# Delta rule of a gated DeltaNet layer: keys and queries of a sample sequence against its states in one 32-column matmul, and the keys' scale on VectorE

## The chip, the cores and the metric

One Trainium2 chip, of which the program uses one core. A core has TensorE (matmuls; loading the stationary operand is shown apart), VectorE, ScalarE, GpSimd and SyncE, each with its own instruction stream, an on-chip memory of 128 partitions (SBUF) and an accumulator memory for matmul results (PSUM, in banks). The metric is the device time of one execution in microseconds (us); lower is better.

## The reference, cut to what matters

Two decoder layers are run for a prompt (1 sequence of 256 positions) and for 8 sample sequences of 4 positions each, which share the weights. The first layer mixes by retention, the second by a gated delta rule; each is followed by a convolutional feed-forward layer. The change lies in the delta rule alone. For one chunk of it:

```python
q = jnp.repeat(l2norm(q), rep, axis=2) * GDN_DK ** -0.5      # 8 key heads, 16 value heads, 128 wide
k = jnp.repeat(l2norm(k), rep, axis=2)
...
G = jnp.cumsum(gc, axis=-1)
dG = G[..., :, None] - G[..., None, :]
decay = jnp.exp(jnp.where(tri_incl, dG, -jnp.inf))
kb = kc * bc[..., None]
L = jnp.where(tri_strict, jnp.einsum('bhid,bhjd->bhij', kb, kc) * decay, 0.0)
rhs = jnp.concatenate([vc * bc[..., None], kb * jnp.exp(G)[..., None]], axis=-1)
sol = lax.linalg.triangular_solve(eye + L, rhs, left_side=True, lower=True, unit_diagonal=True)
u, w = sol[..., :dv], sol[..., dv:]
v_new = u - jnp.einsum('bhid,bhdv->bhiv', w, S)
attn = jnp.einsum('bhid,bhjd->bhij', qc, kc) * decay
o = jnp.einsum('bhid,bhdv->bhiv', qc * jnp.exp(G)[..., None], S) + jnp.einsum('bhij,bhjv->bhiv', attn, v_new)
S = S * jnp.exp(G_last)[..., None, None] + jnp.einsum('bhjd,bhjv->bhdv', kc * jnp.exp(G_last[..., None] - G)[..., None], v_new)
```

The prompt starts from zero states; each of the 8 sample sequences brings its own 128 x 128 state for each of the 16 value heads, and its 4 positions are one chunk.

## The kernel before, in words

**Stages.** The program runs the retention layer, its feed-forward layer, the delta-rule layer (`gdn`), the second feed-forward layer and an end. The delta-rule layer takes about 580 to 985 us of the profiled span. The activations of all 288 positions (256 of the prompt, then 32 of the samples: 8 sequences by 4) stand as columns, so a projection is a chain of matmuls `128x128` by `128x288`, in three passes (`whi` by high part, `whi` by low part, `wlo` by high part), all recorded under the line of `product` (L535). The weights come by DMA, ScalarE rounds them (`whi`, L416) and VectorE makes the rest (`wlo`, L417).

**Order.** The 16 value heads go in four head groups g = 0 to 3, of 4 value heads and 2 key heads. A written list gives the order of the groups' projections: keys and queries (K), values (V), output gate (Z) and output product (D, whose matmuls are called `down`), as `K0 V0 K1 A0 Z0 V1 K2 Z1 V2 K3 D0 V3 Z2 D1 D2 Z3 D3`. Beside it run side tasks, generators that are moved on by one step after every 6 matmuls of a projection (`QUANTUM`). They do the scores, the triangular inverse, the values, the samples and the states. So the side work of one group lies between the projection matmuls of others, and a scheduler then orders the instructions of each engine. TensorE runs its stream in that order: when a side matmul waits, the projection matmuls behind it wait too.

**The steps that the change touches.** `gdn_gates` runs once: it makes the log decays and their sums `pg` by small matmuls, `exs` by an exponential on ScalarE, and `nexg`, the negative of 4 of its columns, by one VectorE instruction (L1096). `gdn_kq` copies each group's sample keys (s = 0) and queries (s = 1) to `kqd`, once for each value head (L1147, GpSimd). `gdn_norms` makes the inverse norms `krs` (L557 is the last instruction of the inverse root, VectorE), then the product `knm` (L1187, VectorE), and the keys' scale `ksc`, beta over the squared norm: 4 GpSimd instructions (L1194) and a fifth for its negative (L1195). `gdn_scores` reads `ksc` first at `gnn` (L1291, VectorE): it multiplies the key scores `pa` (TensorE, L1288, twice for a group) by scale and decay. The second `pa` is put in the same banks and waits for the readers of the first, of which the last are called `gat` (L1295, L1296).

`gdn_samples` handles the 8 sample sequences of a group. The 32 sample columns are position times 8 plus sequence. It spreads the keys and the queries into 8 matrices that hold one sequence's 4 columns and zeros elsewhere (`bigs`, L1462, 4 GpSimd products with a mask of 128x256), so that each matmul writes all 32 columns' rows and the sum over the 8 sequences puts each row right. The states `gS` come by DMA, two sequences at a time. For each sequence bb, for keys and queries (s) and for each of 4 value heads (v) there is one matmul `pks` (L1479):

```python
pks[32 * v : 32 * v + 32, s * P : (s + 1) * P], lhsT=kqm[s][:, v // 2, bb, :], rhs=S[bb // 2][:, bb % 2, v, :]
```

It is 8 x 2 x 4 = 64 matmuls for a group, in 4 bursts of 16. Then `r` is made from the half of the keys (L1486, VectorE, all of this called `t` in the profile) and `qg` from the half of the queries (L1488, ScalarE). Three rounds follow of a small matmul `psy` (L1493) and a VectorE sum. `pks`, `psy` and two more tiles (tag "c") share one PSUM bank, so the first `psy` waits until `r` and `qg` have read `pks`.

`gdn_finish` normalises the outputs: `ro` by the inverse root and `qs` (4 GpSimd instructions at L1621 and one at L1622), `bigc` from it (L1631, VectorE, twice), then the state product `gpS` (L1636, TensorE, 4 matmuls, in one of the two banks of tag "b"). The samples' output is transposed by TensorE (`pxs`, L1660).

Of the kernel before, what the change touches and what calls it, by code (L numbers as in the profile page):

```python
# [295 lines left out]
class Program:  # L296
# [725 lines left out]
    def gdn_gates(self, hs):  # L1022
# [4 lines left out]
        baT = self.big([P, T], F32, "s", 512, 3, 1)[0:32]  # L1027
# [715 lines left out]
```

## Time and profile before

| | us |
|---|---|
| three runs | 1225.26, 1239.33, 1236.23 (median 1236.23) |
| the profiled execution | 1233.65 |
| its span in the trace | 1231.9 |
| TensorE, VectorE, ScalarE, GpSimd busy | 1164.1 (95%), 870.3 (71%), 608.8 (49%), 327.7 (27%) |
| mean granted clock of TensorE, as a share of full speed | 0.972 |

The span lies within the profiled execution's own time; 1.75 us lie around it. Busy times overlap, since the engines run side by side. A matmul in fp32 has two records in the trace, so 64 `pks` of a group are 128 records. Rows of a timeline give start, length, engine, line, operation, output and inputs, and in brackets how long the engine had stood idle just before, and what ended that.

### The profile page before, as it was taken

How to read it: one execution, taken by the hardware profiler on the slowest of the kernel's cores; microseconds unless marked ns; L12 is line 12 of the kernel's file. 1: busy time of each engine (PE TensorE's matmuls, PEld its weight loads, DVE VectorE, ACT ScalarE, POOL GpSimd, SP SyncE). 2: the span in 40 equal slices, each digit the busy share in tenths (PEclk: the TensorE clock that was granted, in tenths of full speed). 3: DMA queues.
4: the chain of work that ended last, by engine and by line, in shares of the span. 5: the costliest groups of instructions: out<-in, count | busy, mean ns of one | idle time of the engine just before them, and what ended most of it. 6: DMA issues, size and time to landing. Idle time of an engine off the chain costs nothing.

```text
span 1231.9 us, 24934 instructions
## 1 busy us (share of the span) xinstructions
PE 1164.1 (95%) x9486; PEld 1049.1 (85%) x9486; DVE 870.3 (71%) x2003; ACT 608.8 (49%) x1256; POOL 327.7 (27%) x507
## 2 busy tenths in 40 slices
PE   6999999999999999999989998988899899999996
PEld 2879798797969999997777788977889699999996
DVE  3657574765766666667679888797965588777775
ACT  2444534344445544444674645744544365555553
POOL 0213142251302122222252223233222113223232
PEclk9999999999999999999999988988989899999998
DMA  9998696877699556557636641533434897777621
GB/s 365 345 332 324 227 336 233 313 246 242 211 314 393 189 171 190 171 181 259 209 92 211 223 144 63 159 129 115 131 103 129 298 357 239 258 254 253 196 76 56
DMA packets 97480, 269.08 MB, mean 218 GB/s; under 512 B 26816, under 2 KB 29088, under 8 KB 97232
## 3 DMA queue, kind: packets, MB, share of 16 engines
q1 hardware_dynamic: 87456, 234.57, 57.2%
q0 software_dynamic: 8032, 29.16, 6.3%
q10 hardware_dynamic: 1872, 3.76, 0.8%
q8 instruction: 75, 1.23, 0.4%
q14 instruction: 45, 0.37, 0.1%
HBM read 236.06 MB, written 31.39 MB: 217 GB/s over the span
## 4 chain that ended last, share of the span: by engine, by line
PE 78%; DVE 12%; DMA 3%; ACT 3%; issue 2%; POOL 1%; SPq 0%; POOLq 0%; ACTq 0%; DVEq 0%
PE down L535 17%; PE fg L535 12%; PE fv L535 12%; PE pg L535 4%; PE pv L535 4%; PE adaP L455 4%; PE p L535 3%; PE gv L535 2%; PE gz L535 2%; DVE wlo L417 2%; DVE mp L1332 2%; PE gk L535 2%; PE pO L898 1%; PE pU L917 1%; PE pS L868 1%
## 5 line engine op out<-in xcount | busy, mean ns | idle before, releaser
L417 DVE TENSOR_TENSOR wlo<-more,whi 128x1024 fp32r<-128x1024 f32 x138 | 171.1, 1241 | 74.5 <-ACT whi L416 63.2
L416 ACT CAST whi<-more 128x1024 fp32r<-128x1024 f32 x138 | 144.3, 1047 | 136.5 <-PE down L535 53.1
L417 DVE TENSOR_TENSOR wlo<-raw,whi 128x1024 fp32r<-128x1024 f32 x123 | 155.4, 1267 | 70.6 <-ACT whi L416 48.4
L416 ACT CAST whi<-raw 128x1024 fp32r<-128x1024 f32 x123 | 128.1, 1044 | 133.5 <-PE down L535 32.8
L716 POOL TENSOR_TENSOR x<-x,dt 128x32 f32<-128x32 f32 x159 | 100.6, 634 | 135.2 <-DVE dt L714 134.1
L712 DVE SCALAR_TENSOR_TENSOR x<-down,mod,x 128x256 f32<-128x256 f32 x160 | 76.6, 479 | 51.3 <-PE down L535 50.5
L591 POOL TENSOR_TENSOR fal<-cv,fah 128x288 fp32r<-128x288 f32 x44 | 41.6, 945 | 215.7 <-ACT fah L590 180.7
L535 PE MATMUL down<-fal,whi 128*128 128x288 f32 x352 | 64.0, 294 | 0.0
L535 PE MATMUL down<-fah,whi 128*128 128x288 f32 x352 | 62.3, 294 | 0.0
L535 PE MATMUL down<-fah,wlo 128*128 128x288 f32 x352 | 62.1, 294 | 0.0
L535 PE MATMUL fg<-hh_ffn,whi 128*128 128x288 f32 x352 | 58.9, 300 | 1.2 <-ACT hh_ffn L637 1.2
L918 DVE SCALAR_TENSOR_TENSOR S<-S,pU 128x512 f32<-128x512 f32 x64 | 42.2, 684 | 24.2 <-PE pU L917 24.1
L535 PE MATMUL fv<-hh_ffn,whi 128*128 128x288 f32 x352 | 58.7, 298 | 0.0
L535 PEld LDWEIGHTS fg<-hh_ffn,whi 128*128 128x128 f32 x352 | 50.6, 189 | 5.6 <-ACT hh_ffn L646 2.6
L535 PE MATMUL fg<-hh_ffn,wlo 128*128 128x288 f32 x352 | 55.0, 296 | 0.0
L535 PE MATMUL fv<-hh_ffn,wlo 128*128 128x288 f32 x352 | 54.8, 295 | 0.0
L535 PE MATMUL fv<-hl_ffn,whi 128*128 128x288 f32 x352 | 54.3, 295 | 0.0
L535 PE MATMUL fg<-hl_ffn,whi 128*128 128x288 f32 x352 | 54.0, 295 | 0.0
L535 PEld LDWEIGHTS fv<-hh_ffn,whi 128*128 128x128 f32 x352 | 50.5, 189 | 2.5 <-ACT ftail L947 1.2
L535 PEld LDWEIGHTS down<-fah,whi 128*128 128x128 f32 x352 | 51.8, 188 | 0.8 <-ACT whi L416 0.4
L535 PEld LDWEIGHTS down<-fal,whi 128*128 128x128 f32 x352 | 52.3, 188 | 0.2 <-issue 0.2
L535 PEld LDWEIGHTS down<-fah,wlo 128*128 128x128 f32 x352 | 52.0, 188 | 0.0
(492 smaller groups left out, 2923.4 us busy)
## 6 DMA issues: line engine op xcount, KB each, us to landing
raw<-in_wada SPq DMA_DIRECT2D x69, 512.0 KB, 4.9
more<-in_wu SPq DMA_DIRECT2D x68, 512.0 KB, 4.9
raw<-in_wgi SPq DMA_DIRECT2D x48, 512.0 KB, 3.9
more<-in_wada SPq DMA_DIRECT2D x43, 512.0 KB, 5.9
more<-in_wd SPq DMA_DIRECT2D x41, 512.0 KB, 4.4
S<-in_sr SPq DMA_DIRECT2D x16, 1024.0 KB, 8.0
out_rs<-S POOLq DMA_DIRECT2D x16, 1024.0 KB, 8.1
raw<-in_wri SPq DMA_DIRECT2D x28, 512.0 KB, 4.9
```

The costliest lines, as they stand in the source:

```text
L416: nc.scalar.copy(hi[:, :c], r)
L417: nc.vector.tensor_tensor(lo[:, :c], r, hi[:, :c].bitcast(F32), ALU.subtract)
L455: nc.tensor.matmul(self.adaP[32 * g : 32 * g + 32, 0:256], lhsT=self.cs[:, k, :], rhs=rv[:, :, g, :], start=(k == 0), stop=(k == KT - 1), ...
L535: self.nc.tensor.matmul(out, lhsT=av[:, k, c0 : c0 + m], rhs=b[:, k, :], start=(k0 == 0 and i == 0), stop=(k1 == kts and i == len(seq) - 1))
L591: (nc.gpsimd if pool_lo else nc.vector).tensor_tensor(lo, src, hi.bitcast(F32), ALU.subtract)
L712: nc.vector.scalar_tensor_tensor(xm[:, :TP], p[:, :TP], g[:, 0:1], xm[:, :TP], ALU.mult, ALU.add)
L716: (nc.vector if gate == 11 and last and m == KT - 1 else nc.gpsimd).tensor_tensor(xv, xv, t, ALU.add)
L868: nc.tensor.matmul(pS, lhsT=kt[:, j, c * P : (c + 1) * P], rhs=vt[:, j, :], start=(j == 0), stop=(j == 1))
L898: nc.tensor.matmul(pO4[32 * g : 32 * g + 32, :], lhsT=qm[:, c, 4 * bb + g, :], rhs=S[bb, c][:, g, :], start=(bb == 0 and c == 0), stop=Fal ...
L917: nc.tensor.matmul(pU, lhsT=kms[g][:, c * P : (c + 1) * P], rhs=vst, start=True, stop=True)
L918: nc.vector.scalar_tensor_tensor(S[bb, c][:, g, :], S[bb, c][:, g, :], gamma4, pU, ALU.mult, ALU.add)
L1332: nc.vector.tensor_tensor(m, Ti[:, 0:k, :].rearrange("p j c -> p c j").unsqueeze(1).to_broadcast([P, w, 8, k]), X[:, 0:k, i:k].rearrange(" ...
```

## The change

It has six parts, all in the delta-rule layer.

1. **One matmul for keys and queries of a sequence.** `kqm` is a tile of its own, twice (for even and odd groups), set to zero once. Of sequence bb, the 32 columns hold its 4 key columns at its own places and its 4 query columns at the places of the sequence that is 4 further or nearer. Six strided GpSimd copies a group fill it, in place of the 4 products with the mask. Sequences 0 to 3 write the first half of `pks` and 4 to 7 the second, so each half holds keys of its own four sequences and queries at the others' places. There are 8 x 4 = 32 matmuls for a group, of the same shape as before, in 4 bursts of 8.
2. **Reading both halves.** `r` takes two VectorE instructions, one for each half, with a scale that is zero where the half holds queries. `qg` takes a ScalarE copy of the first half and a VectorE instruction that adds the second. The queries' places are exchanged by halves, so `kqd`, `du` and `ident_q` are built with their halves exchanged: 4 GpSimd copies of 128x32 a group instead of 2 of 128x64, `du` in two products instead of one.
3. **Gates.** `pg` gets a third product with the exchanged constant, `exs` 12 columns instead of 8, and `nexg` becomes four sets of 4 columns, made with two masks.
4. **The keys' scale on VectorE.** `ksc` is made by three VectorE instructions in place of the five on GpSimd.
5. **The output's inverse scale `qs`** takes one GpSimd instruction instead of 4, and `pxs` is a matmul with `ident_q` instead of a transpose.
6. **Buffers.** The tag "bigs" has 2 buffers instead of 3.

```diff
@@ gdn @@
+            self.kqm = t("kqm", [P, 2, 2, 33 * NB])
+            nc.gpsimd.memset(self.kqm, 0.0)
+            self.ident_q = t("ident_q", [P, P])
@@ gdn_gates @@
+        sq = self.big([P, P], F32, "s", 512, 2, 1)
+        for f in range(2):
+            nc.vector.tensor_copy(self.half(sq, f), self.half(self.cst("supto"), 1 - f))
+            nc.vector.tensor_copy(self.half(self.ident_q, f), self.half(self.ident, 1 - f))
+        nc.tensor.matmul(pg[:, 8:12], lhsT=sq, rhs=gs, start=True, stop=True)
...
-        self.exs = t("exs", [P, 8])
-        nc.scalar.activation(self.exs, pg[:, 0:8], AF.Exp)
+        self.exs = t("exs", [P, 12])
+        nc.scalar.activation(self.exs, pg[:, 0:12], AF.Exp)
...
-        nc.vector.tensor_scalar(nexg, self.exs[:, 0:4], -1.0, None, ALU.mult)
+        mk, nexg = t("mlh", [P, 2]), t("nexg", [P, 4, 4])
+        for f in range(2):
+            nc.vector.tensor_reduce(mk[:, f : f + 1], self.cst("pmask")[:, 4 * f : 4 * f + 4], AX.X, ALU.add)
+        for f in range(2):
+            nc.vector.tensor_scalar(nexg[:, f], self.exs[:, 0:4], mk[:, f : f + 1], -1.0, ALU.mult, ALU.mult)
+            nc.vector.tensor_scalar(nexg[:, 2 + f], self.exs[:, 8:12], mk[:, 1 - f : 2 - f], None, ALU.mult)
@@ gdn_norms @@
-        for jt in range(2):
-            for j in range(2):
-                bsl = self.beta[:, jt, 4 * g + 2 * j : 4 * g + 2 * j + 2]
-                c = 2 * jt + j
-                nc.gpsimd.tensor_scalar(sc[:, 1, jt, 2 * j : 2 * j + 2], bsl, rr[:, c : c + 1], rr[:, c : c + 1], ALU.mult, ALU.mult)
-        nc.gpsimd.tensor_scalar(sc[:, 0], sc[:, 1], -1.0, None, ALU.mult)
+        r2 = t("kr2", [P, 4], bufs=2)
+        nc.vector.tensor_tensor(r2, rr[:, 0:4], rr[:, 0:4], ALU.mult)
+        by_h = lambda v: v.rearrange("p t (j h) -> p t j h", h=2)
+        nc.vector.tensor_tensor(
+            by_h(sc[:, 1]), by_h(self.beta[:, 0:2, 4 * g : 4 * g + 4]),
+            r2.rearrange("p (t j) -> p t j", j=2).unsqueeze(3).to_broadcast([P, 2, 2, 2]), ALU.mult
+        )
+        nc.vector.tensor_scalar(sc[:, 0], sc[:, 1], -1.0, None, ALU.mult)
@@ gdn_samples @@
-        kqm = [big([P, 2, NB, TS]) for _ in range(2)]
-        for s in range(2):
-            for j in range(2):
-                nc.gpsimd.tensor_tensor(kqm[s][:, j], kqd[:, s, 2 * j, :].unsqueeze(1).to_broadcast([P, NB, TS]), bm, ALU.mult)
+        kqm = self.kqm[:, g % 2]
+        by_b = lambda v, b0, n: v.rearrange("p (t b) -> p b t", b=NB)[:, b0 : b0 + n, :]
+        for j in range(2):
+            km, q = kqm[:, j].rearrange("p (b x) -> p b x", x=33), a["kqT"][:, j, 1, TP:]
+            nc.gpsimd.tensor_copy(km[:, :, 0 : TS - NB + 1 : NB], by_b(a["kqT"][:, j, 0, TP:], 0, NB))
+            nc.gpsimd.tensor_copy(km[:, 0:4, 4 : TS - 3 : NB], by_b(q, 0, 4))
+            km = kqm[:, j, P : P + 132].rearrange("p (b x) -> p b x", x=33)
+            nc.gpsimd.tensor_copy(km[:, :, 0 : TS - NB + 1 : NB], by_b(q, 4, 4))
...
-            for s in range(2):
-                for v in range(4):
+            s = bb // 4
+            for v in range(4):
+                nc.tensor.matmul(
+                    pks[32 * v : 32 * v + 32, s * P : (s + 1) * P], lhsT=kqm[:, v // 2, TS * bb : TS * (bb + 1)], rhs=S[bb // 2][:, bb % 2, v, :],
...
-        nc.vector.scalar_tensor_tensor(r, pks[:, 0:P], self.nexg[:, g : g + 1], vs, ALU.mult, ALU.add)
-        qg = small()
-        nc.scalar.activation(qg, pks[:, P : 2 * P], AF.Copy, scale=self.exs[:, g : g + 1])
+        for s in range(2):
+            ps, x = pks[:, s * P : (s + 1) * P], self.nexg[:, s, g : g + 1]
+            nc.vector.scalar_tensor_tensor(r, ps, x, r if s else vs, ALU.mult, ALU.add)
+        nc.scalar.activation(qg, pks[:, 0:P], AF.Copy, scale=self.nexg[:, 2, g : g + 1])
+        nc.vector.scalar_tensor_tensor(qg, pks[:, P : 2 * P], self.nexg[:, 3, g : g + 1], qg, ALU.mult, ALU.add)
@@ gdn_finish @@
-        for it in range(2):
-            for j in range(2):
-                nc.gpsimd.tensor_scalar(qs[:, 4 * it + 2 * j : 4 * it + 2 * j + 2], self.ones[:, 0:2], rr[:, 4 + 2 * it + j : 5 + 2 * it + j], f, ALU.mult, ALU.mult)
+        nc.gpsimd.tensor_scalar(qs[:, 0:8].rearrange("p (c h) -> p c h", h=2), rr[:, 4:8].unsqueeze(2).to_broadcast([P, 4, 2]), f, None, ALU.mult)
...
-        nc.tensor.transpose(px[:, 0:P], ons, self.ident)
+        nc.tensor.matmul(px[:, 0:P], lhsT=ons, rhs=self.ident_q, start=True, stop=True)
```

The lines below shift: `gnn` stands at L1321 to L1323 in the changed kernel, `pks` at L1512, `r` at L1521, `qg` at L1523, `psy` at L1528, `bigc` at L1664 and `gpS` at L1669.

The first place is VectorE's order at the scores of group 0, from `knm` to the first `gnn`; before:

```order
L1187 TENSOR_TENSOR knm_7209<-kss_6914,krs_7197 128x10
L1455 TENSOR_SCALAR ssc_7571<-bs,krs_7197 128x1
L1456 TENSOR_SCALAR ssc_7571<-ssc_7571 128x1
L1457 TENSOR_SCALAR ssc_7571<-ssc_7571,exs 128x1
L1291 SCALAR_TENSOR_TENSOR gnn_7225<-pa_7263,ksc_7211,gat_6973 128x128
L1292 SCALAR_TENSOR_TENSOR gnn_7225<-pa_7263,gat_6973 128x128
```

and with the change (`kr_0` is the tile of squared inverse norms, `ssc` a scale of the samples):

```order
L1215 TENSOR_TENSOR knm_7226<-kss_6917,krs_7214 128x10
L1219 TENSOR_TENSOR kr_0_7229<-krs_7214 128x4
L1484 TENSOR_SCALAR ssc_7587<-bs,krs_7214 128x1
L1221 TENSOR_TENSOR ksc_7228<-beta,kr_0_7229 128x8
L1485 TENSOR_SCALAR ssc_7587<-ssc_7587 128x1
L1486 TENSOR_SCALAR ssc_7587<-ssc_7587,exs 128x1
L1225 TENSOR_SCALAR ksc_7228<-ksc_7228 128x8
L1321 SCALAR_TENSOR_TENSOR gnn_7241<-pa_7279,ksc_7228,gat_6988 128x128
L1322 SCALAR_TENSOR_TENSOR gnn_7241<-pa_7279,gat_6988 128x128
```

The three instructions of the scale now stand between `knm` and the first `gnn`, mixed with those of `ssc`, and nothing of GpSimd is awaited there.

The second place is TensorE's order around the state product `gpS` of the third group (group 2). `gz` are gate projections and `down` the output product. Before:

```order
L1479 MATMUL pks_10661<-gS_10712,bigs 32x128 x16
L535 MATMUL gz_10731<-hh_gdn,wlo 128x288 x6
L535 MATMUL gz_10837<-hh_gdn,whi 128x288 x3
L1636 MATMUL gpS_10714<-bigc,kn_8400 128x256 x4
L1479 MATMUL pks_10661<-gS_10754,bigs 32x128 x16
L535 MATMUL gz_10837<-hh_gdn,whi 128x288 x5
L535 MATMUL gz_10837<-hl_gdn,whi 128x288 x7
L1493 MATMUL psy_10878<-t_3_10820,t_3_10655 128x128
L535 MATMUL gz_10837<-hl_gdn,whi 128x288
L535 MATMUL gz_10837<-hh_gdn,wlo 128x288 x8
```

and with the change:

```order
L1512 MATMUL pks_10588<-gS_10628,kqm 32x128 x8
L535 MATMUL gz_10647<-hh_gdn,wlo 128x288 x2
L535 MATMUL gz_10731<-hh_gdn,whi 128x288 x6
L1512 MATMUL pks_10588<-gS_10662,kqm 32x128 x8
L535 MATMUL gz_10731<-hh_gdn,whi 128x288 x2
L535 MATMUL gz_10731<-hl_gdn,whi 128x288 x8
L535 MATMUL gz_10731<-hh_gdn,wlo 128x288 x8
L535 MATMUL down<-gah_9789,whi 128x288 x3
L1669 MATMUL gpS_10630<-bigc,kn_8388 128x256 x4
L535 MATMUL down<-gah_9789,whi 128x288
L535 MATMUL down<-gal_9790,whi 128x288 x4
L535 MATMUL down<-gah_9789,wlo 128x288
```

The bursts of `pks` have 8 matmuls instead of 16, and `gpS` has moved back: it stood behind the first 3 matmuls of a `gz` chain, and now stands behind all 24 of that chain and 3 of `down`.

The third place is VectorE's order in group 1 between the end of the `pks` bursts and `bigc`. `Ti`, `mp` belong to the triangular inverse of another group, `gcv` to its convolution. Before:

```order
L1336 TENSOR_REDUCE Ti_8254<-mp_8306 128x16
L557 SCALAR_TENSOR_TENSOR ro_8686<-rsu_o_8688,ro_8686 128x9
L1486 SCALAR_TENSOR_TENSOR t_1_8725<-pks_8536,nexg,gvs_8165 128x128
L1338 SCALAR_TENSOR_TENSOR Ti_8254<-Ti_8254,xp_8261 128x8
L1628 TENSOR_TENSOR ro_8686<-ro_8686,qs_8677 128x9
L1111 SCALAR_TENSOR_TENSOR gcv<-gk_8603,prm_b,gcv 128x255
L1332 TENSOR_TENSOR mp_8306<-Ti_8254,X_8253 128x16x19
L1631 TENSOR_TENSOR bigc<-po_8551,ro_8686 128x512
```

and with the change:

```order
L1521 SCALAR_TENSOR_TENSOR t_1_8679<-pks_8525,nexg,gvs_8153 128x128
L555 SCALAR_TENSOR_TENSOR rsu_o_8650<-rsu_o_8650,rsv_o_8649 128x9
L1368 SCALAR_TENSOR_TENSOR Ti_8242<-Ti_8242,xp_8249 128x8
L556 SCALAR_TENSOR_TENSOR rsu_o_8650<-rsu_o_8650 128x9
L1521 SCALAR_TENSOR_TENSOR t_1_8679<-pks_8525,nexg,t_1_8679 128x128
L557 SCALAR_TENSOR_TENSOR ro_8648<-rsu_o_8650,ro_8648 128x9
L1127 SCALAR_TENSOR_TENSOR gcv<-gk_8584,prm_b,gcv 128x255
L1661 TENSOR_TENSOR ro_8648<-ro_8648,qs_8642 128x9
L1523 SCALAR_TENSOR_TENSOR t_1_8680<-pks_8525,nexg,t_1_8680 128x128
L1664 TENSOR_TENSOR bigc<-po_8540,ro_8648 128x512
```

`r` is now two instructions with three others between them, and a third read of `pks`, the second part of `qg`, stands four rows behind the second and ahead of both `bigc`.

## Rows read from the trace of the kernel before

**Rows 1.** The page: the span, the busy time of the engines, and the shares of the chain of waits that ended last, by engine.

```profile
span 1231.9 us, 24934 instructions
...
PE 1164.1 (95%) x9486; PEld 1049.1 (85%) x9486; DVE 870.3 (71%) x2003; ACT 608.8 (49%) x1256; POOL 327.7 (27%) x507
...
PE 78%; DVE 12%; DMA 3%; ACT 3%; issue 2%; POOL 1%; SPq 0%; POOLq 0%; ACTq 0%; DVEq 0%
```

**Rows 2.** The table of busy times for the delta-rule stage. Columns: stretch and its length, then busy time (instructions) of TensorE, weight load, VectorE, ScalarE, GpSimd, then granted clock, DMA share, GB/s.

```profile
590.00:985.00 395.00, 355.55 (x3191) 317.99 (x3192) 306.74 (x819) 214.80 (x547) 116.51 (x218) 0.94 0.50 153
```

**Rows 3.** Waits of TensorE in the same stretch: waiting line, line waited for, us in total, times, longest.

```profile
PE pa L1288 <- DVE gat L1295: 7.3, 4, 2.2
PE gpS L1636 <- DVE bigc L1631: 5.8, 3, 4.3
PE pks L1479 <- DMA gS<-in_sg: 3.2, 3, 1.7
PE psy L1493 <- ACT t L1488: 2.6, 2, 2.4
```

**Rows 4.** Groups of instructions by form in the same stretch: `pks` on TensorE. Columns: busy us, mean ns of one record, then idle before them and its causes.

```profile
L1479 PE MATMUL pks<-gS,bigs 128*32 128x128 f32 x512 | 18.3, 285 | 3.5 <-DMA gS<-in_sg 3.2
```

**Rows 5.** Timeline of group 3, from `knm`, made of the inverse norms, to the first `gnn`.

```profile
839.58 0.17 DVE L1187 TENSOR_TENSOR knm<-kss,krs 128x10 f32<-128x10 f32 x1
839.65 2.34 POOL L1194 TENSOR_SCALAR ksc<-beta,krs 128x2 f32<-128x2 f32 x4 [0.54 <-DVE dt L714]
...
842.08 0.25 POOL L1195 TENSOR_SCALAR ksc<-ksc 128x8 f32<-128x8 f32 x1
...
842.37 0.35 DVE L1291 SCALAR_TENSOR_TENSOR gnn<-pa,ksc,gat 128x128 f32<-128x128 f32 x1 [1.47 <-POOL ksc L1195]
```

**Rows 6.** Timeline of VectorE, the first `gnn` of groups 0, 1 and 2.

```profile
627.53 0.35 DVE L1291 SCALAR_TENSOR_TENSOR gnn<-pa,ksc,gat 128x128 f32<-128x128 f32 x1 [2.77 <-POOL ksc L1195]
...
680.85 0.35 DVE L1291 SCALAR_TENSOR_TENSOR gnn<-pa,ksc,gat 128x128 f32<-128x128 f32 x1 [1.47 <-POOL ksc L1195]
...
762.45 0.35 DVE L1291 SCALAR_TENSOR_TENSOR gnn<-pa,ksc,gat 128x128 f32<-128x128 f32 x1 [1.38 <-POOL ksc L1195]
```

**Rows 7.** Timeline of TensorE, the second `pa` of the four groups.

```profile
629.70 1.12 PE L1288 MATMUL pa<-kqT 128*128 128x512 f32 x2 [1.75 <-DVE gat L1295]
...
683.02 1.13 PE L1288 MATMUL pa<-kqT 128*128 128x512 f32 x2 [1.54 <-DVE gat L1295]
...
764.72 1.10 PE L1288 MATMUL pa<-kqT 128*128 128x512 f32 x2 [1.84 <-DVE gat L1295]
...
844.54 1.33 PE L1288 MATMUL pa<-kqT 128*128 128x512 f32 x2 [2.19 <-DVE gat L1295]
```

**Rows 8.** Groups by form, the two readers of `pks` (columns as in rows 4).

```profile
L1488 ACT ACTIVATE t<-pks,exs 128x128 f32<-128x128 f32 x4 | 1.5, 368 | 6.3 <-DVE t L1486 6.2
...
L1486 DVE SCALAR_TENSOR_TENSOR t<-pks,nexg,gvs 128x128 f32<-128x128 f32 x4 | 1.4, 342 | 1.7 <-PE pks L1479 1.7
```

**Rows 9.** Timeline of group 1, from `r` to the first `psy`.

```profile
731.88 0.34 DVE L1486 SCALAR_TENSOR_TENSOR t<-pks,nexg,gvs 128x128 f32<-128x128 f32 x1
732.14 0.21 DVE L1338 SCALAR_TENSOR_TENSOR Ti<-Ti,xp 128x8 f32<-128x8 f32 x1
732.25 0.37 ACT L1488 ACTIVATE t<-pks,exs 128x128 f32<-128x128 f32 x1 [3.19 <-DVE t L1486]
...
732.35 0.47 DVE L1111 SCALAR_TENSOR_TENSOR gcv<-gk,prm_b,gcv 128x255 f32<-128x255 f32 x1
...
732.67 0.80 PE L1493 MATMUL psy<-t,t 128*128 128x128 f32 x2 [2.39 <-ACT t L1488]
```

**Rows 10.** The table of busy times around `gpS` of the third group, in stretches of 5 us (columns as in rows 2).

```profile
890.00:895.00 5.00, 1.01 (x3) 0.87 (x4) 5.00 (x15) 0.00 (x0) 2.00 (x5) 0.81 0.41 158
895.00:900.00 5.00, 5.00 (x41) 3.52 (x40) 3.32 (x7) 0.59 (x1) 0.61 (x1) 0.51 0.31 81
```

**Rows 11.** A piece of the chain of waits: a run of projection matmuls, start and length.

```profile
943.23 12.81 PE gz L535 x96
```

**Rows 12.** Groups by form, the GpSimd instructions that the change touches (columns as in rows 4).

```profile
L1462 POOL TENSOR_TENSOR bigs<-kqd,cst_b 128x256 f32<-128x256 f32 x16 | 14.0, 880 | 1.1
...
L1147 POOL COPY kqd<-kqT 128x64 f32<-128x64 f32 x16 | 8.9, 559 | 45.9 <-ACT kqT L1114 45.8
```

**Rows 13.** Timeline of GpSimd at the start of the layer: a zeroing, and `baq`, made of what ScalarE copied.

```profile
589.11 0.95 POOL L987 MEMSET TT<- 128x1024 f32 x1 [8.02 <-PE adaP L455]
...
592.20 0.98 POOL L1030 COPY baq<-bigs 32x128 f32<-32x128 f32 x1 [1.68 <-ACT bigs L1028]
```

**Rows 14.** Timeline of TensorE at the gates: one of the small matmuls `pg`.

```profile
608.21 0.36 PE L1081 MATMUL pg<-gs,cst_g 128*128 128x4 f32 x2
```

**Rows 15.** Timeline of TensorE: a `psy`, which is an fp32 matmul of 128x128, and the transpose `pxs`.

```profile
819.26 0.38 PE L1493 MATMUL psy<-t,t 128*128 128x128 f32 x2
...
820.71 0.27 PE L1660 MATMUL pxs<-cst,ons 128*128 128x128 f32 x1
```

**Rows 16.** Groups by form, long VectorE instructions of the same stretch (columns as in rows 4).

```profile
L417 DVE TENSOR_TENSOR wlo<-raw,whi 128x1024 fp32r<-128x1024 f32 x64 | 78.4, 1229 | 26.8 <-ACT whi L416 20.2 <-issue 2.4 <-PE gk L535 2.2
...
L1631 DVE TENSOR_TENSOR bigc<-po,ro 128x512 f32<-128x512 f32 x8 | 5.3, 679 | 0.0
...
L1332 DVE TENSOR_TENSOR mp<-Ti,X 128x496 f32<-128x496 f32 x4 | 4.5, 1118 | 0.0
```

More of the change, by code (lines that the diff above doesn't have):

```diff
@@ L978, in gdn @@
             nc.vector.tensor_copy(self.ident_r, self.ident)
-            nu = gp.tile([P, 512], F32, tag="bigs", name="nu", bufs=3)[:, 0:384]
+            nu = gp.tile([P, 512], F32, tag="bigs", name="nu", bufs=2)[:, 0:384]
             nc.scalar.dma_start(nu, self.A["not_upto"])
@@ L1026, in gdn_gates @@
         pb = self.pba
[L1027 removed]
+        baT = self.big([P, T], F32, "s", 512, 2, 1)[0:32]
         nc.scalar.copy(baT, pb[0:32, 0:T])
@@ L1146, in gdn_kq @@
                 self.gdn_conv(g, 2 * s + j, p, halo, kqT[:, j, s, :])
-                nc.gpsimd.tensor_copy(kqd[:, s, 2 * j : 2 * j + 2, :], kqT[:, j, s, TP:].unsqueeze(1).to_broadcast([P, 2, TS]))
+                if s:
+                    for f in range(2):
+                        nc.gpsimd.tensor_copy(
+                            self.half(kqd[:, 1, 2 * j : 2 * j + 2, :].rearrange("p h t -> p (h t)"), f).rearrange("p (h t) b -> p h t b", h=2),
+                            self.half(kqT[:, j, 1, TP:], 1 - f).unsqueeze(1).to_broadcast([P, 2, TD, 4]),
+                        )
+                else:
+                    nc.gpsimd.tensor_copy(kqd[:, s, 2 * j : 2 * j + 2, :], kqT[:, j, s, TP:].unsqueeze(1).to_broadcast([P, 2, TS]))
                 if s:
@@ L1155, in gdn_kq, with half @@
         d["sqd"] = sqd
+    def half(self, v, f):
+        return v.rearrange("p (t f b) -> p t f b", f=2, b=4)[:, :, f, :]
     def gdn_norms(self, g, d):
@@ L1468, in gdn_samples @@
         nc.gpsimd.tensor_tensor(db, ds_, self.cst("sbefore"), ALU.mult)
-        nc.gpsimd.tensor_tensor(du, ds_, self.cst("supto"), ALU.mult)
+        for f in range(2):
+            nc.gpsimd.tensor_tensor(self.half(du, f), self.half(ds_, 1 - f), self.half(self.cst("supto"), 1 - f), ALU.mult)
         nc.vector.scalar_tensor_tensor(db, pas[:, 0:P], sc[:, 1:2], db, ALU.mult, ALU.mult)
@@ L1475, in gdn_samples @@
                 yield
-            for s in range(2):
-                for v in range(4):
-                    nc.tensor.matmul(
-                        pks[32 * v : 32 * v + 32, s * P : (s + 1) * P], lhsT=kqm[s][:, v // 2, bb, :], rhs=S[bb // 2][:, bb % 2, v, :],
-                        start=(bb == 0 and s == 0), stop=(bb == NB - 1 and s == 1), skip_group_check=True,
-                    )
+            s = bb // 4
+            for v in range(4):
+                nc.tensor.matmul(
+                    pks[32 * v : 32 * v + 32, s * P : (s + 1) * P], lhsT=kqm[:, v // 2, TS * bb : TS * (bb + 1)], rhs=S[bb // 2][:, bb % 2, v, :],
+                    start=(bb == 0), stop=(bb == NB - 1), skip_group_check=True,
+                )
             if bb % 2 and bb < 4:
                 load(bb // 2 + 2)
-        r = small()
-        nc.vector.scalar_tensor_tensor(r, pks[:, 0:P], self.nexg[:, g : g + 1], vs, ALU.mult, ALU.add)
-        qg = small()
-        nc.scalar.activation(qg, pks[:, P : 2 * P], AF.Copy, scale=self.exs[:, g : g + 1])
+        r, qg = small(), small()
+        for s in range(2):
[3 more added lines that the diff above has]
+        nc.vector.scalar_tensor_tensor(qg, pks[:, P : 2 * P], self.nexg[:, 3, g : g + 1], qg, ALU.mult, ALU.add)
         y = r
```

6 lines of the change are left out of this document (2 added, 4 removed).

## The prediction

> **What bounds the kernel now.** I read the page first: TensorE is busy for 1164.1 of 1231.9 us, and the chain that ended last runs through it for 78%, VectorE for 12%, GpSimd for 1% [rows 1]. So the kernel is a stream of matmuls with few gaps, and a change is worth what it takes from that stream or from the gaps in it. The whole change lies in the delta-rule stage, so next comes the table of that stretch: in 395 us TensorE is busy for 355.6, idle for 39.4, VectorE is busy for 306.7 (78%), GpSimd for 116.5 (30%) [rows 2]. The reader is to see two numbers: at most 39 us of idle can be had back, and VectorE has little room. The waits say which of the idle the change can reach: `pa` for VectorE's `gat` 7.3 us, `gpS` for `bigc` 5.8, `pks` for the state loads 3.2, `psy` for `qg` 2.6 [rows 3]. That is 18.9 us, about half.
>
> **Half of the pks matmuls.** 512 records, two for a matmul, make 256 matmuls, 18.3 us of TensorE [rows 4]. The new matmuls have the same shape and are 128, so 9.2 us of work go. How much of it shortens the stream? Three of the 16 bursts stand behind a state load [rows 3]; a burst that is shorter there leaves the next load where it was. I take the 13 others in full: 9.15 x 13/16 = **-7.4**. Bounds: 0 (all of it becomes a longer wait elsewhere) and -9.2.
>
> **The keys' scale on VectorE.** In group 3 the four GpSimd instructions take 2.34 us and the fifth 0.25, while VectorE waits 1.47 us for them ahead of the first `gnn` [rows 5]; in groups 0 to 2 it waits 2.77, 1.47 and 1.38 [rows 6], 7.1 in all. Three small VectorE instructions take the place; the nearest row, `knm` of 128x10, is 0.17 [rows 5], so 0.51 of each wait comes back, and 2.26, 0.96, 0.87 and 0.96 go. VectorE then frees the scores' banks sooner, and TensorE's second `pa`, which waits 1.75, 1.54, 1.84 and 2.19 [rows 7], starts sooner by as much, but never by more than it waits. That caps group 0 at 1.75: 1.75 + 0.96 + 0.87 + 0.96 = **-4.5**. Bounds: 0 and -7.1. Neither queue loses by it: GpSimd has 70% of the stage free [rows 2].
>
> **More reading on VectorE.** A group has two more reads of `pks` on VectorE, 8 in all, of the kind of `r`, 0.342 us [rows 8]: 2.7 us. What of it is felt is not shown by a row; I take VectorE's busy share of 78% [rows 2], **+2.1**. Bounds: 0 and +2.7.
>
> **The bank of pks is held longer.** The first `psy` writes into the one bank of `pks`, so it can't start before `qg` is there. Before, in group 1, `r` starts at 731.88 and `qg` ends at 732.62, 0.74 us later, since ScalarE works beside VectorE [rows 9]. In the changed order nine VectorE instructions stand from the first part of `r` to the last part of `qg`: three reads of 0.342, one `Ti` step of 0.21 and one `gcv` of 0.47 [rows 8, 9] and four small ones of 0.17 [rows 5], 2.39 us. That is 1.65 more, of which 0.53 (two reads, by 78%) is in the term above: **+1.1**. In the other three groups I take none, since `psy` has projection matmuls ahead of it. Bounds: -2.6 (the whole wait of `psy` goes, because the bursts end sooner) and +4.5 (all four groups pay 1.65, less the 2.1 above).
>
> **The third state product.** The longest wait of `gpS` is 4.3 us [rows 3]. In the changed order it stands behind 21 more `gz` matmuls; I leave out the three `down`, which may themselves wait. A projection matmul takes 12.81/96 = 0.133 [rows 11], so 2.8 us of work fill the gap, and VectorE reaches `bigc` later by two reads, 0.68: **-2.1**. Bounds: 0 and -4.3. Work moved into a gap is gained only if nothing opens where it came from.
>
> **Gates, transpose, GpSimd.** The gates gain a matmul of 0.36 [rows 14] and nine small VectorE instructions of 0.17, 1.9 us once; `nexg` is first read much later, so I take **+0.5** (0 to +1.9). The transpose `pxs` is one record of 0.27; an fp32 matmul with the same operands is two, 0.38 [rows 15]: 4 x 0.11 = **+0.4**. On GpSimd 4 products of 0.880 a group [rows 12] become 6 small copies, and 2 copies of queries become 4 of half the size; the engine is 70% idle, so 0 both ways. If that cover were gone, two more copies of 0.559 [rows 12] a group would cost 4.5 at most, and the products that leave pay for it. The zeroing of `kqm`, about the size of the one that takes 0.95, lies beside `baq`'s wait of 1.68 for ScalarE [rows 13]: 0. Two "bigs" buffers instead of three cost 0, because their largest users leave.
>
> **Sum.** -7.4 - 4.5 + 2.1 + 1.1 - 2.1 + 0.5 + 0.4 = -9.9, against the profiled execution's 1233.65: 1223.75, so **1224 us**. The median of the three runs is 2.6 higher than that execution; against 1236.23 the same step would give 1226.3.
>
> **A stretch at half clock.** Around the long wait of `gpS` TensorE is busy for 1.01 us out of 5, and in the next 5 us, busy throughout, its granted clock is 0.51 of full, that is the lower of its two levels, 1.2 GHz, where 5 x 0.49 = 2.45 us are lost [rows 10]. The Trainium skill ("TensorE: Matmul & The Clock Gate", section "HAM oscillation — how this bites in real kernels") says that a TensorE left idle is throttled to half clock, and that the burst of matmuls behind the gap pays for it. The trace agrees, with the 0.51 behind that gap. By that rule shorter bursts may cost as well as save: where work is taken out and the wait behind it stays, the gap is longer. This is the second rival.
>
> **The rivals.**
>
> *Larger.* All of the 9.15 of `pks` count, the 7.1 before `gnn` and the 4.3 of `gpS` go in full, and without that gap the half-clock stretch behind it goes too, 2.45. With the four additions (2.1 + 1.1 + 0.5 + 0.4 = 4.1): -9.15 - 7.1 - 4.3 - 2.45 + 4.1 = -18.9, **1215**. For it: these waits are of VectorE on TensorE's stream, and the scale stands directly ahead of them. Against: all must go at once, while VectorE gets more work.
>
> *Idle instead of work.* The time of the saved matmuls becomes idle before the same waits, and the clock falls twice more for about 5 us: -9.9 + 7.4 + 2 x 2.45 = +2.4, **1236**. For it: the stage already runs at 0.94 [rows 2]. Against: 13 of 16 bursts wait for nothing.
>
> *Slower.* The second part of `qg` waits in VectorE's queue behind long work, and with it the only bank of `pks` and TensorE's `psy`. A weight split of 1.23, an inverse product of 1.12 and two `bigc` of 0.68 [rows 16] ahead of it make 3.7 us a group: -9.9 + 4 x 3.7 = +4.9, 1239. It decides from (9.9 + 12.3)/4 = 5.6 us a group on, that is with one and a half times that work ahead of the read: **1246** or more. For it: ScalarE read that half before, with 54% of the stage to this engine busy [rows 2], and VectorE is the busier. Against: in the order shown only `gcv` and small ones stand there, and `bigc` behind.
>
> *No gain.* The steps do as they say, but the order that the scheduler finds afresh puts TensorE's gaps elsewhere, and the stage ends where it did: **1233**. For it: each gap is a meeting of two streams, and all are shifted. Against: `gnn`'s wait goes whatever the order.
>
> **How the numbers follow.** Forecast 0.46 (its own range 1217 to 1230, the sum with its larger terms at half or in full), larger 0.24, idle 0.17, slower 0.07, no gain 0.06. A change of about 1%, 12.3 us, is what a measurement of this kernel can tell from none. Faster is below 1221.3: the larger case and a quarter of the forecast's, 0.24 + 0.12 = 0.36. Slower is the third rival alone, 0.07. The rest, 0.57, is within 1%. The range 1213 to 1238 leaves out the slower case, a quarter of the larger and a fifth of the idle case, 0.07 + 0.06 + 0.03 = 0.16.
>
> **What would show it.** In the changed profile: 256 records of `pks` with about 9.2 us; no wait of `gnn` for the scale, and waits of the second `pa` shorter by 0.9 to 1.8 each; VectorE busier in the stage by 2.7 us and three small instructions a group; first `psy` waiting up to 2.4 us behind the last read of `pks` in group 1; `gpS` of the third group waiting about 2 us. The larger case shows TensorE at full clock behind that `gpS`; the idle case shows TensorE's idle grown by about 7 us and more slices at 0.5; the slower case shows `psy` waiting for VectorE by over 5 us in each group. I am wrong if the stage from the first gate matmul to the last `down` changes by less than 4 us or more than 17.

## The result, and the profile after

The changed kernel takes 1219.49 us (median of 4 runs, 1217.6 to 1221.22), the kernel before 1233.23 beside it: ratio 0.9894 with a 95% interval of 0.9864 to 0.9923, that is 13.1 us less (9.5 to 16.8). Two more sets of runs, made beside the experiments, gave 0.9875 and 0.9890. The forecast was -9.9 us, 1224, and the range holds the time.

The page of the changed kernel:

```profile
span 1215.8 us, 24453 instructions
...
PE 1150.0 (95%) x9236; PEld 1036.6 (85%) x9236; DVE 872.7 (72%) x2032; ACT 609.1 (50%) x1256; POOL 316.2 (26%) x496
...
PE 76%; DVE 13%; DMA 5%; ACT 3%; issue 2%; POOL 1%; SPq 0%; POOLq 0%; ACTq 0%; DVEq 0%
```

TensorE is busy for 14.1 us less than in [rows 1], and the span is 16.1 us shorter in these two single executions. Outside the delta-rule stage nothing moves: it starts at 580.7 in both traces, and behind it 244.7 and 244.3 us follow. The stage from 580 us to the first matmul of the next feed-forward layer, before and then changed (columns as in rows 2):

```profile
580.00:987.22 407.22, 366.33 (x3314) 324.03 (x3306) 315.89 (x841) 221.67 (x562) 119.00 (x220) 0.93 0.51 159
```

```profile
580.00:971.48 391.48, 352.45 (x3065) 311.76 (x3057) 318.75 (x870) 222.09 (x562) 107.96 (x209) 0.97 0.53 166
```

It is 407.22 us before and 391.48 now, 15.7 less. TensorE's busy time falls by 13.9, and its **idle time hardly, in this pair of executions: 40.9 before, 39.0 now**. The granted clock rises from 0.93 to 0.97, and VectorE's work by 2.9, about the 2.7 that was counted. Of the 13.9, the product has 7.0 (below); the other 6.9 come from matmuls that are the same but for a few, at the higher clock. What TensorE waits for now:

```profile
PE pe L1388 <- DVE uc L1377: 3.9, 1, 3.9
...
PE gpS L1669 <- DVE Ti L1368: 3.0, 1, 3.0
PE psy L1528 <- DVE t L1523: 2.6, 1, 2.6
...
PE pks L1512 <- issue: 2.0, 1, 2.0
...
PE pvs L1457 <- ACT gvt L1453: 1.8, 1, 1.8
PE pks L1512 <- DMA gS<-in_sg: 1.6, 3, 0.8
...
PE psy L1528 <- DVE t L1530: 1.3, 2, 0.9
PE pd L1289 <- POOL decay L1275: 1.3, 1, 1.3
...
PE pa L1318 <- DVE gat L1325: 0.6, 1, 0.6
```

Against [rows 3] the second `pa` has gone from 7.3 us to 0.6 and `gpS` from 5.8 to 3.0. But `pe` waits 3.9 for the inverse (`uc`), `pks` 3.6 in two rows instead of 3.2, `psy` 3.9 in two rows instead of 2.6, `pvs` 1.8 and `pd` 1.3. Two of these waited before, too:

```profile
PE pe L1358 <- DVE uc L1347: 2.5, 2, 2.2
...
PE pd L1259 <- ACT kqT L1114: 0.8, 1, 0.8
```

The waits that the change aimed at went; in this pair of executions others grew in their place.

The product itself, by form (columns as in rows 4):

```profile
L1512 PE MATMUL pks<-gS,kqm 128*32 128x128 f32 x256 | 11.3, 288 | 3.7 <-issue 2.0 <-DMA gS<-in_sg 1.6
```

256 records as forecast, and 11.3 us where 18.3 stood in [rows 4]: 7.0 less, not the 9.15 of the sum. A burst of 16 matmuls before, and one of 8 now:

```profile
656.90 1.08 PE L1479 MATMUL pks<-gS,bigs 128*32 128x128 f32 x32
```

```profile
655.26 0.64 PE L1512 MATMUL pks<-gS,kqm 128*32 128x128 f32 x16
```

Half of the matmuls take more than half of the time: 0.44 less for each of 16 bursts make the 7.0. The scale of group 0, from `knm` to the second `pa`:

```profile
625.82 0.17 DVE L1215 TENSOR_TENSOR knm<-kss,krs 128x10 f32<-128x10 f32 x1
...
625.90 0.18 DVE L1219 TENSOR_TENSOR kr<-krs 128x4 f32<-128x4 f32 x1
...
626.19 0.15 DVE L1221 TENSOR_TENSOR ksc<-beta,kr 128x8 f32<-128x8 f32 x1
...
626.49 0.16 DVE L1225 TENSOR_SCALAR ksc<-ksc 128x8 f32<-128x8 f32 x1
...
626.77 0.35 DVE L1321 SCALAR_TENSOR_TENSOR gnn<-pa,ksc,gat 128x128 f32<-128x128 f32 x1
...
629.38 1.07 PE L1318 MATMUL pa<-kqT 128*128 128x512 f32 x2
```

The three instructions take 0.18, 0.15 and 0.16, with those of `ssc` between, and `gnn` starts 0.95 us after `knm` without a wait, where VectorE waited 2.77 in [rows 6]. The second `pa` has no bracket any more; it waited 1.75 in [rows 7]. Yet it starts only 0.32 us earlier than in [rows 7] (629.38 against 629.70). The bank of `pks` in group 1:

```profile
728.19 0.34 DVE L1521 SCALAR_TENSOR_TENSOR t<-pks,nexg,gvs 128x128 f32<-128x128 f32 x1
...
728.75 0.34 DVE L1521 SCALAR_TENSOR_TENSOR t<-pks,nexg,t 128x128 f32<-128x128 f32 x1
...
729.55 0.34 DVE L1523 SCALAR_TENSOR_TENSOR t<-pks,nexg,t 128x128 f32<-128x128 f32 x1
...
730.03 0.46 PE L1528 MATMUL psy<-t,t 128*128 128x128 f32 x2 [2.63 <-DVE t L1523]
```

From the start of `r` to the end of `qg` it is 1.70 us (728.19 to 729.89), 0.74 in [rows 9] and 2.39 forecast. `psy` waits 2.63 for it, 2.39 before. Around `gpS` of the third group (columns as in rows 2):

```profile
880.00:885.00 5.00, 2.15 (x5) 1.81 (x6) 5.00 (x12) 0.67 (x2) 0.47 (x2) 0.79 0.33 105
885.00:890.00 5.00, 5.00 (x33) 4.67 (x33) 3.90 (x11) 1.52 (x2) 0.75 (x2) 0.87 0.43 129
```

TensorE is busy for 2.15 of 5 us, and the clock falls to 0.79 and 0.87 in these two stretches, where [rows 10] had 1.01 of 5, 0.81 and 0.51.

### The profile page after: what moved, and what is told of

Its sections match the earlier page's. It is cut to its first block, busy times and chain, and to the rows that moved or that the text cites. A ratio compares the mean times of both kernels' runs of the same rounds, so it can differ in the third digit from the quotient of the medians.

```text
span 1215.8 us, 24453 instructions
## 1 busy us (share of the span) xinstructions
PE 1150.0 (95%) x9236; PEld 1036.6 (85%) x9236; DVE 872.7 (72%) x2032; ACT 609.1 (50%) x1256; POOL 316.2 (26%) x496
## 4 chain that ended last, share of the span: by engine, by line
PE 76%; DVE 13%; DMA 5%; ACT 3%; issue 2%; POOL 1%; SPq 0%; POOLq 0%; ACTq 0%; DVEq 0%
PE down L535 17%; PE fg L535 12%; PE fv L535 12%; PE pg L535 4%; PE pv L535 4%; PE adaP L455 4%; PE p L535 3%; PE gv L535 3%; DVE wlo L417 3%; DVE mp L1362 2%; PE pO L898 1%; PE pU L917 1%; DVE Ti L1366 1%; PE gk L535 1%; PE pe L1388 1%
## 5 line engine op out<-in xcount | busy, mean ns | idle before, releaser
L716 POOL TENSOR_TENSOR x<-x,dt 128x32 f32<-128x32 f32 x159 | 103.1, 650 | 135.0 <-DVE dt L714 134.2
```

The costliest lines, as they stand in the source:

```text
L716: (nc.vector if gate == 11 and last and m == KT - 1 else nc.gpsimd).tensor_tensor(xv, xv, t, ALU.add)
```

## The experiments

Twelve sets of runs on three chips (four rows of the table each), two of them of the changed kernel again, each beside the kernel before on its chip. The us are the ratio's distance from 1 times that kernel's median there (1231.77, 1230.34, 1231.36), negative for faster. Stage, busy and idle are TensorE's in one profiled execution, from 580 us to the first matmul of the next layer. The stage's own first matmul starts between 580.6 and 582.9, so up to 2.3 us of stage and busy lie ahead of it; idle is the same from either start.

| kernel | ratio (95%) | us | stage, busy, idle |
|---|---|---|---|
| scale_only | 0.9945 (0.9923 to 0.9966) | -6.8 | 397.2, 358.7, 38.5 |
| half_pks | 0.9938 (0.9916 to 0.9960) | -7.6 | 398.8, 355.3, 43.5 |
| no_scale | 0.9956 (0.9939 to 0.9973) | -5.4 | 401.1, 356.6, 44.5 |
| pks_twice | 0.9923 (0.9898 to 0.9949) | -9.5 | 400.2, 361.5, 38.7 |
| changed_again | 0.9875 (0.9850 to 0.9901) | -15.4 | 397.1, 357.1, 39.9 |
| one_read | 0.9908 (0.9888 to 0.9928) | -11.3 | 392.7, 351.9, 40.7 |
| psy_other_bank | 0.9920 (0.9900 to 0.9939) | -9.8 | 395.1, 355.4, 39.6 |
| qs_only | 1.0021 (1.0006 to 1.0037) | +2.6 | 407.3, 361.3, 46.0 |
| changed_third | 0.9890 (0.9854 to 0.9926) | -13.5 | 393.9, 357.8, 36.1 |
| reads_more | 0.9943 (0.9911 to 0.9975) | -7.0 | 398.3, 356.3, 42.0 |
| pks_four | 1.0143 (1.0112 to 1.0174) | +17.6 | 420.1, 400.6, 19.5 |
| qs_four | 0.9910 (0.9877 to 0.9943) | -11.1 | 400.9, 360.0, 40.9 |

**The scale, alone and left out.** `scale_only` puts the new lines of `gdn_norms` into the kernel before, `no_scale` puts the old ones into the changed kernel:

```diff
...
-                nc.gpsimd.tensor_scalar(sc[:, 1, jt, 2 * j : 2 * j + 2], bsl, rr[:, c : c + 1], rr[:, c : c + 1], ALU.mult, ALU.mult)
...
+        nc.vector.tensor_tensor(r2, rr[:, 0:4], rr[:, 0:4], ALU.mult)
...
```

> The kernel before with the keys' scale alone moved to VectorE (three instructions). Theory of the terms: VectorE's wait for the scale goes, and TensorE's second pa starts earlier, -4.5 us, ratio 0.996 to the kernel before; TensorE's idle in the delta-rule stage falls from 39.4 to about 35 us. Rival, the waits only move: pa waits go, others of the same total come, idle stays at 38 to 41 us, ratio 1.000 unless the number of half-clock stretches changes; each stretch of some 5 us at the lower level is worth about 2.5 us.

> The changed kernel with the keys' scale put back on GpSimd (five instructions). Theory of the terms: 4.5 us slower than the changed kernel, ratio to the kernel before 0.993. Rival, the waits only move: as the changed kernel, 0.989, with pa waits of about 7 us back and other waits smaller.

Alone it brings 6.8 us (4.2 to 9.5), more than the 4.5 of the sum, which lies inside. The changed kernel without it keeps 5.4 (3.3 to 7.5), in the middle what the sum had left over, -9.9 + 4.5. The parts add up within these intervals: 6.8 + 5.4 = 12.2 beside 13.1 to 15.4. So the forecast of that wait was right and on the small side. The rival that waits only move is wrong on the time. Taken alone, the profile of `scale_only` seems to be for it:

```profile
PE gpS L1638 <- DVE Ti L1340: 4.1, 1, 4.1
...
PE gpS L1638 <- DVE bigc L1633: 3.9, 2, 3.0
...
PE pa L1290 <- DVE gat L1297: 0.8, 2, 0.6
```

`pa` waits 0.8 us in all, 7.3 in [rows 3], and `gpS` 8.0 instead of 5.8; idle is 38.5 beside 40.9. But one execution each is too few: `qs_only` (below), which runs the order of the kernel before, idles for 46.0. The other three kernels with the scale on GpSimd, `qs_only`, `half_pks` and `no_scale`, wait like this for `pa`:

```profile
PE pa L1288 <- DVE gat L1295: 7.1, 4, 2.2
```

```profile
PE pa L1288 <- DVE gat L1295: 6.0, 3, 2.5
```

```profile
PE pa L1316 <- DVE gat L1323: 5.0, 2, 2.8
```

Sorted by the scale, the idle times differ: 40.9 (the kernel before), 46.0, 43.5 and 44.5, on average 43.7, with it on GpSimd, and 36.1 to 42.0, on average 39.5, in the nine executions with it on VectorE (`pks_four` left out), whatever else was edited. The 4.2 between them are about the 4.5 of the sum. The sorting was made after the runs, and the two groups overlap between 40.9 and 42.0.

**The product, halved, twice and four times.** `half_pks` takes the loop of 32 matmuls into the kernel before, so half of the product is left out; `pks_twice` and `pks_four` issue each matmul of the changed kernel 2 and 4 times, so the product counts double and fourfold:

```diff
@@ half_pks @@
-            for s in range(2):
-                for v in range(4):
+            s = bb // 4
+            for v in range(4):
...
@@ pks_twice; range(4) in pks_four @@
+                for n in range(2):
...
```

> The kernel before with half of the pks matmuls: sequences 0 to 3 only for the keys, 4 to 7 only for the queries, so half of that product is left out; nothing else changes, and no read is added. Theory of the terms: -7.4 us (0 to -9.2), ratio 0.994, pks busy about 9.2 us. Rival, the saved work becomes idle: TensorE busy falls by 9 but its idle in the stage rises by as much, ratio 1.000.

> The changed kernel with each pks matmul issued twice into the same sums (so the product counts double), 64 a group as before the change; the reads, the scale and the rest are as changed. Theory of the terms: 7.4 us slower than the changed kernel (up to 9.2), ratio to the kernel before 0.9955. Rival, most of the gain came with fewer half-clock stretches: the ratio follows the time at the lower clock, not the 9.2 us; if the four stretches of the changed kernel stay four, the cost is about 9, and if they become seven, about 16.

> The changed kernel with each pks matmul issued four times into the same sums (the product counts fourfold), 128 a group: 27 us more of TensorE than the changed kernel has. Theory of the terms: 13/16 of it is felt, 22 us slower than the changed kernel, ratio 1.006. If, as with each issued twice, only half is felt because the clock falls less often and waits are filled, 13 us, ratio 0.999.

The product halved in the kernel before, and issued twice in the changed one:

```profile
L1479 PE MATMUL pks<-gS,bigs 128*32 128x128 f32 x256 | 10.1, 278 | 4.2 <-DMA gS<-in_sg 4.0
```

```profile
L1513 PE MATMUL pks<-gS,kqm 128*32 128x128 f32 x512 | 19.9, 281 | 3.9 <-DMA gS<-in_sg 2.1 <-issue 1.6
```

Halved alone it brings 7.6 us (4.9 to 10.3) for 8.2 us of TensorE less (10.1 instead of 18.3); -7.4 was forecast. From the other side the price comes out smaller: issued twice it costs TensorE 8.6 us more (19.9 against 11.3) and the run about 4.5 (0.9923 against 0.9886, the mean of the three sets of the changed kernel). The intervals leave 1 to 8 us there, so the 7.4 is not excluded from this side either. The saved time doesn't turn to idle: with the scale on GpSimd, the two kernels with half of the product idle for 43.5 and 44.5, the two with the whole for 40.9 and 46.0. Issued four times:

```profile
L1513 PE MATMUL pks<-gS,kqm 128*32 128x128 f32 x1024 | 70.1, 276 | 0.0
```

```profile
580.00:1000.05 420.05, 400.55 (x3837) 362.13 (x3829) 321.62 (x869) 221.82 (x562) 102.25 (x209) 0.99 0.52 154
```

My expectation had the dose wrong: it was to be 27 us more of TensorE, and it is 58.8 (70.1 against 11.3). Beside the burst of 8 above (0.64 us), these are the same eight issued twice in a row, and four times:

```profile
657.58 1.12 PE L1513 MATMUL pks<-gS,kqm 128*32 128x128 f32 x32
```

```profile
654.49 4.33 PE L1513 MATMUL pks<-gS,kqm 128*32 128x128 f32 x64
```

0.64 us for 8 matmuls is 0.08 each, 1.12 for 16 is 0.07, 4.33 for 32 is 0.135. In the changed kernel, neighbours write to different 32 rows of the output; of four issued in a row, all write to the same. The Trainium skill ("TensorE: Matmul & The Clock Gate", section "Measured speedup vs the span model") gives 2.38 times the speed for three matmuls packed into different 32-column tiles of the array. The bursts of 8 and of four in a row agree with that, but two in a row write to the same rows as well and cost no more than the 1.08 of 16 different ones, so the cause of the 0.135 stays open. What holds without it: 58.8 us of matmuls more cost 31.1 (17.6 + 13.5), about half. In the same execution TensorE's idle is 19.5, 36.1 in the changed kernel's on that chip, and the clock stays at 0.99, where that execution has:

```profile
580.00:973.88 393.88, 357.76 (x3088) 316.02 (x3081) 319.95 (x873) 222.50 (x563) 108.19 (x209) 0.95 0.53 165
```

So of the 58.8, 16.6 us fill waits, and 16.0 come back because the other matmuls, the same in number but for those ahead of the stage (about 1 us), are shorter at the higher clock (330.4 against 346.4); 26.2 remain as a longer stage.

**The reads of pks and its bank.** `one_read` takes the second reads away (half of each sum is left out), `reads_more` adds four a group, whose results are overwritten, `psy_other_bank` gives `psy` other banks:

```diff
@@ one_read @@
...
+        nc.vector.scalar_tensor_tensor(r, pks[:, 0:P], self.nexg[:, 0, g : g + 1], vs, ALU.mult, ALU.add)
+        nc.scalar.activation(qg, pks[:, P : 2 * P], AF.Copy, scale=self.nexg[:, 3, g : g + 1])
@@ reads_more @@
+        for s in (0, 1, 0, 1):
+            nc.vector.scalar_tensor_tensor(qg, pks[:, s * P : (s + 1) * P], self.nexg[:, 2 + s, g : g + 1], vs, ALU.mult, ALU.add)
@@ psy_other_bank @@
-            py = self.aux(f"psy{g}{n}", "c")
+            py = self.aux(f"psy{g}{n}", "b")
```

> The changed kernel with r made from the first half of pks alone (one VectorE instruction) and qg from the second alone (ScalarE), as many reads as before the change, so half of each sum is left out. Theory of the terms: 3.2 us faster than the changed kernel (2.1 for VectorE's work, 1.1 for the bank), ratio to the kernel before 0.9865, and the wait of the first psy in group 1 falls from 2.6 us to under 1. Rival, the reads lie beside other work and the wait is that of a burst that ends late: ratio 0.989 as the changed kernel, and the psy wait stays over 2 us, as it was 2.4 before the change.

> The changed kernel with four more VectorE reads of pks for each group ahead of qg, whose results are overwritten: 16 more of 0.34 us, 5.5 us of VectorE. It is twice the dose of what the change added, in the same place. Theory of the terms (VectorE's busy share of 78% is felt, and the bank is held longer): 4.3 us for the work and up to 4 x 1.4 for the bank, 4 to 10 us slower than the changed kernel, ratio 0.992 to 0.996. Rival, such reads lie beside other work as the run with one read suggested: under 2 us slower, 0.988 to 0.990.

> The changed kernel with psy in the two banks of tag b instead of the one of pks, so that the first psy no longer waits until qg has read pks (it needs r alone). If the bank held by qg costs what the sum says, 1 to 2 us faster than the changed kernel, ratio 0.988, and the wait of psy for qg is gone. If r itself is what comes late, psy waits for r in its place and the time stays, 0.989; if tag b then delays the others that use it, slower by 1 to 3 us.

The two doses of reads disagree. Sixteen more cost 6.5 us beside the changed kernel on the same chip (0.9943 against 0.9890; the intervals leave 1 to 12), as the sum would have it; eight fewer brought nothing, it is 4 us slower than the changed kernel (0.9908 against 0.9875; 0 to 8), where 3.2 faster was forecast. The waits of `one_read` say where it went:

```profile
PE psy L1525 <- ACT t L1520: 4.1, 2, 2.6
...
PE psy L1525 <- DVE t L1527: 2.3, 2, 1.4
```

`psy` now waits 4.1 us for the ScalarE copy, more than the 2.6 for VectorE's read: a shorter list of reads didn't shorten the wait for the bank. So the price of 3.2 us for reads and bank was not found as such. With `psy` in other banks:

```profile
PE pks L1512 <- DMA gS<-in_sg: 3.7, 3, 2.2
PE gpS L1669 <- DVE Ti L1368: 3.1, 1, 3.1
...
PE gpS L1669 <- DVE bigc L1664: 2.7, 1, 2.7
...
PE psy L1528 <- DVE t L1530: 0.4, 1, 0.4
```

`psy` waits 0.4 us instead of 3.9, the wait is gone as expected; but `gpS` waits 5.8 instead of 3.0, `pks` 3.7 for its states, idle is 39.6, and the run is 5.5 us slower than the changed kernel on that chip (0.9920 against 0.9875; 2 to 9).

**An edit that was to cost nothing.** `qs_only` puts the single GpSimd instruction for `qs` into the kernel before, `qs_four` the four old ones into the changed kernel:

```diff
...
+        nc.gpsimd.tensor_scalar(qs[:, 0:8].rearrange("p (c h) -> p c h", h=2), rr[:, 4:8].unsqueeze(2).to_broadcast([P, 4, 2]), f, None, ALU.mult)
```

> The kernel before with only the output's inverse scale qs made by one GpSimd instruction instead of four, which the sum counts at nothing. By the terms: ratio 1.000. It also shows what a reshuffled order is worth by itself, since the scheduler finds its order afresh: if steps of 3 us or more come from that alone, this run moves by as much, either way. Against: the four stand in the line to bigc that gpS waits for, 1.3 us a group, and gpS waits 5.8 us in all, so up to -4 us, 0.9965, if that line decides.

> The changed kernel with the output's inverse scale qs made by four GpSimd instructions as before. By the terms 0, ratio as the changed kernel. If the slower result of the kernel before with only this edit was the edit's own, this version is 2 to 3 us faster than the changed kernel, 0.986, and beats both; if it was the reshuffled order, the sign can be either.

Fewer instructions, and the kernel before is 2.6 us slower (0.7 to 4.6). Put back into the changed kernel, the four don't make it faster (0.9910 against 0.9890 on the same chip, intervals that overlap). The profiled executions of `qs_only` and of the kernel before don't show the 2.6: both spans are 1231.9 us, and the stage of `qs_only` is

```profile
580.00:987.29 407.29, 361.32 (x3342) 320.55 (x3340) 320.94 (x844) 221.96 (x563) 114.79 (x208) 0.96 0.51 160
```

407.29 beside 407.22. Nor did a new order come of it: from end to end of these two traces, TensorE, VectorE and ScalarE run through the same sequence of operations, as far as the timelines have it (one short TensorE row stands in one of them only), and GpSimd's differs at `qs` alone; so it is with `qs_four` and the changed kernel. So these two runs do not show what a new order is worth, as the expectations meant them to, and no other run shows it by itself, since the other edits change order and work together. What made the 2.6 stays open. The three sets of the changed kernel, with one order, lie 2.3 us apart, so differences of that size can't be read here. No version beat the changed kernel. Its repeats:

> The changed kernel once more, for its clocks beside the others. Both theories: ratio 0.989 with a spread of 0.003. If the lower clock of some runs is what spreads them, a run's time should go up by about 0.4 to 0.6 us for each us that its mean granted clock loses.

> The changed kernel again, as the one that the next three are to be compared with on the same chip. Ratio 0.988, spread 0.003.

The spread between the sets is as expected. Pooled over the 140 runs, within each kernel and chip, a run is 0.47 us longer for each us that its clock loses (time by one less granted clock). The kernel before has a mean clock of 0.976 (50 runs), the changed one 0.980 (14 runs): 1232 x 0.0239 = 29.4 us lost against 1218 x 0.0201 = 24.5, which by that slope is 2.3 us of the gain. The slope was fitted after the runs, and a run with longer waits could lose clock by them, so this is an estimate.

## Why the prediction was right, point by point

- **Half of the matmuls, -7.4.** Shown from the kernel before, -7.6. From the changed kernel it is nearer 4.5 (1 to 8). The work that the sum saw saved was too large: it is 7.0 in the changed kernel and not 9.15, since a burst of 8 takes 0.64 us and not half of 1.08. That the 3/16 taken off for the state loads bring the term back to 7.4 is luck; no run shows that share. The rival that saved work turns to idle is not borne out: idle doesn't grow with half of the product.
- **The scale, -4.5.** Right mechanism, small size: -6.8 alone, the `pa` waits gone, and TensorE's idle 4.2 lower on average in the executions with it. I capped each group by its own wait and counted nothing behind it. In group 0 the cap itself didn't hold in this pair of executions; nothing was gained there. The trace up to the end of the first values' projection, before and then changed, and two waits in the changed kernel:

```profile
580.00:637.73 57.73, 50.85 (x382) 43.80 (x374) 44.22 (x132) 39.66 (x95) 23.71 (x41) 0.94 0.48 161
```

```profile
580.00:637.77 57.77, 50.50 (x390) 42.86 (x383) 45.59 (x146) 42.08 (x100) 20.32 (x40) 0.97 0.50 166
```

```profile
PE gv L535 <- DVE gcv L1127: 1.5, 1, 1.5
...
PE pd L1289 <- POOL decay L1275: 1.3, 1, 1.3
```

57.7 us in both, though the `pa` wait of 1.75 is gone: the 1.5 of `gv` is new, and `pd` waits 1.3 instead of 0.8.

- **Reads and bank, +2.1 and +1.1.** VectorE's work is as forecast, +2.9 us. The bank is held 0.96 us longer in group 1 (1.70 instead of 0.74), not 1.65, and the first `psy` waits only 0.24 longer (2.63 instead of 2.39), not 1.1. As a price not confirmed: taking the reads away gave nothing.
- **Third `gpS`, -2.1.** 4.29 before [rows 3, as 4.3], 3.05 now: 1.2 of the 2.1. Behind the 27 matmuls it still waits for VectorE, which has reads and inverse steps ahead of `bigc`.
- **Gates and transpose, +0.9; GpSimd 0.** Too small for any run. `qs` measured +2.6 on the kernel before, where 0 stood, with the order unchanged; terms of 0.5 can't be checked where sets of runs of one kernel lie 2.3 apart.
- **The clock.** The sum had no term for it; I put it into the rivals, up in one and down in the other, and priced a stretch at half clock in full, 2.45; by the slope of 0.47 about 1.2 of that is felt. It went up, by an estimated 2.3 us. With the scale's 2.3 more than forecast this covers the 3.2 between -9.9 and -13.1, but the intervals are wider than that, so the split is not shown.

So the forecast case held, with a piece of the larger case (the `pa` waits went whole, the clock fell less). The idle rival was wrong on both counts: idle did not grow, and the clock did not fall. What did not hold is the sentence that a wait's removal starts TensorE's stream sooner by as much, where it is taken place by place: the second `pa` of group 0 starts 0.32 us sooner for a wait of 1.75, and in `psy_other_bank` a wait of 3.9 fell to 0.4 while idle stayed at 39.6. Summed over the stage it held for the scale, 4.2 of 4.5. In total the terms are right to within what the runs can tell; as far as the errors of single terms cancel in it, that is luck.
